# A four-layer trunk in which the retention's output product is computed head by head by Strassen's algorithm

## Chip, cores and metric

One core of a Trainium2 chip. The metric is the time of one execution of the program in microseconds on the device, the median of three runs; lower is better.

## The reference

Four residual layers; the token mixer of layer i is number i mod 3: retention (layers 0 and 3), a conformer convolution (1), a short gated convolution (2). Each mixer is followed by a squared-ReLU MLP, with a norm ahead of and behind every sublayer. All in float32, 512 tokens of width 1024. What the change touches is the last line of the retention mixer, `y @ w_out`:

```python
def retention_mixer(x, positions, w_in, gn_g, w_out):
    q, k, v, g = jnp.split(x @ w_in, [D_MODEL, 2 * D_MODEL, 2 * D_MODEL + RET_VDIM], axis=-1)
    ...                                   # 4 heads: q, k of 256, v, g of 512 columns each
    q = apply_rotary(q, cos, sin)
    k = apply_rotary(k, cos, sin) * (RET_DK ** -0.5)
    y = chunkwise_retention(q, k, v)      # 512 x 4 x 512
    mean = jnp.mean(y, axis=-1, keepdims=True)
    var = jnp.mean(jnp.square(y - mean), axis=-1, keepdims=True)
    y = ((y - mean) * lax.rsqrt(var + LN_EPS)).reshape(bsz, s, RET_VDIM) * gn_g.astype(F32)
    y = (jax.nn.silu(g.astype(F32)) * y).astype(x.dtype)
    return y @ w_out                      # 512 x 2048 times 2048 x 1024
```

## The kernel before

**Precision.** TensorE multiplies in a reduced float32 format, so every operand is held as a high part and a low part and every product is three matmuls (`mm3`: high by high, high by low, low by high). A high part is a ScalarE copy, the low part a VectorE subtraction of it from the value (`split`; `high` with `flush` is the same with the subtraction put off until the next copy).

**Weights.** `piece_list` writes out by hand the order in which weight pieces of 128 x 1024 are used. `fetch_hi` (ScalarE, line 289 or 284) and `fetch_lo` (VectorE, 302 or 298) split a piece; seven split pieces are held (`W_BUFS`), two raw ones. A piece that is used adds one to `owed`; `settle`, called just ahead of the next use, issues the owed fetches at that place of ScalarE's and VectorE's program. A raw tile is loaded by a DMA on SP's queue when the raw tile two before it has been split. A "fast" piece is no raw tile: it is one of the seven weight forms of a Strassen round and is made from four blocks (`blk`) that lie in SBUF, by VectorE subtractions in place (`combine`, line 329).

**Order.** All five engines run their instructions in the order in which the Python program issues them. PSUM has eight banks, taken in turn.

**Rounds.** `fast_round` multiplies one group by Strassen's algorithm in the Winograd form, with tokens, contraction and output columns each cut in two: seven forms, each of 2 banks x 2 contraction tiles x 3 matmuls = 12 matmuls of 512 columns for a group of four tiles (an ordinary product has 96 for the same, the round 84). Each form's two banks are added into `f` in SBUF at one or two places each (line 1385, or line 1383, a ScalarE copy, where the place is still empty). `halves_of` makes the left forms from a pair of tiles: splits and four sums of 256 columns. `fast_end` makes the last two sums. The MLPs use rounds of 16 and 8 tiles with the last four hidden tiles as a short last round, the short convolution one round of four tiles.

**Retention** goes head by head: query and key tiles of the next head (`do_qk`), scores (`do_s`), the retention product of this head (`do_o`), gate tiles (`gate` of `next(g)`), statistics (`stats`, `newton`, line 895 and 896), four output tiles (`do_y`, lines 829, 831, then the split), the value product of the next head (`do_v`: 96 matmuls, then the evacuations at lines 750, 754, 756). In head 0 the gate tiles were computed earlier, all but one of which stands between `do_o` and the statistics; in heads 1 and 2 one gate tile stands there and three behind the statistics; in head 3 two ahead of `do_o`, one ahead of the statistics and one behind. The output product before: at head 2, heads 0 and 1 together in `out_round` (8 pieces, into `f`); at the end heads 2 and 3 in `out_final`:

```python
        short = len(slots) == 1
        if not short:
            banks = [self.bank() for _ in range(4)]
            for kp in range(4):
                ...
                self.ts_part(banks, piece, slots, kp, mode == "bias")
```

That part takes the left 512 output columns, with head 2's contraction tiles first; after it `block(b)` computes the right 512 columns of each 128 tokens. With one slot (`short`) it falls away and `block(b)` computes both halves of the columns. The norms of the boundary are interleaved with the blocks.

## Time and profile before

| | |
|---|---|
| median of 3 runs | 2529.47 us (2528.72 to 2529.48) |
| the profiled execution, its own time | 2531.34 us |
| its span, first to last instruction | 2529.4 us |
| busy: TensorE, VectorE, ScalarE, GpSimd | 99%, 70%, 49%, 9% |
| mean granted TensorE clock | 0.996 of full |
| DMA moved | 290.97 MB, mean 115 GB/s |

The span is that of one execution with the hardware profiler on; the other 1.9 us of its time lie around it. Busy shares are means over stages that have different limits.

### The profile page before, as it was taken

How to read it: one execution, taken by the hardware profiler on the slowest of the kernel's cores; microseconds unless marked ns; L12 is line 12 of the kernel's file. 1: busy time of each engine (PE TensorE's matmuls, PEld its weight loads, DVE VectorE, ACT ScalarE, POOL GpSimd, SP SyncE). 2: the span in 40 equal slices, each digit the busy share in tenths (PEclk: the TensorE clock that was granted, in tenths of full speed). 3: DMA queues.
4: the chain of work that ended last, by engine and by line, in shares of the span. 5: the costliest groups of instructions: out<-in, count | busy, mean ns of one | idle time of the engine just before them, and what ended most of it. 6: DMA issues, size and time to landing. Idle time of an engine off the chain costs nothing.

```text
span 2529.4 us, 31444 instructions
## 1 busy us (share of the span) xinstructions
PE 2506.8 (99%) x12245; PEld 2121.1 (84%) x12245; DVE 1777.3 (70%) x2361; ACT 1232.6 (49%) x1874; POOL 218.4 (9%) x248
## 2 busy tenths in 40 slices
PE   9999999999999999999999999999999999999998
PEld 8888889888888788888898898888988888888887
DVE  7665346897978978678776577788756534687686
ACT  3553444555446656544443365445444334465543
POOL 0000002000026920000010100000200000200000
PEclk9999999999999999999999999999999999999999
DMA  4323234324243523331332233313332222331313
GB/s 154 111 88 104 84 117 138 138 104 171 90 146 101 192 98 142 133 134 67 141 109 88 87 142 133 133 67 123 124 104 82 95 88 102 136 135 73 133 67 125
DMA packets 85029, 290.97 MB, mean 115 GB/s; under 512 B 9488, under 2 KB 11280, under 8 KB 84880
## 3 DMA queue, kind: packets, MB, share of 16 engines
q1 hardware_dynamic: 84880, 288.96, 32.5%
q8 instruction: 96, 1.57, 0.3%
q14 instruction: 53, 0.43, 0.1%
HBM read 265.79 MB, written 21.50 MB: 114 GB/s over the span
## 4 chain that ended last, share of the span: by engine, by line
PE 64%; DVE 2%; POOL 2%; ACT 1%; issue 1%; DMA 0%; DVEq 0%; POOLq 0%; SPq 0%; ACTq 0%
PE bank L364 12%; PE bank L363 12%; PE bank L366 12%; PE bank L355 9%; PE bank L353 9%; PE bank L354 9%; POOL tiny L423 1%; DVE x L455 1%; POOL tiny L426 0%; PE bank L471 0%; POOL pbuf L1132 0%; DVE xin L404 0%; ACT bnd L442 0%; DMA whi<-phase 0%; PE bank L523 0%
## 5 line engine op out<-in xcount | busy, mean ns | idle before, releaser
L363 PE MATMUL bank<-xin,whi 128*128 128x512 f32 (+1 forms) x2160 | 759.9, 361 | 0.0
L364 PE MATMUL bank<-xin,wlo 128*128 128x512 f32 (+1 forms) x2160 | 757.2, 360 | 1.1 <-DVE wlo L302 1.1
L302 DVE TENSOR_TENSOR wlo<-raw,whi 128x1024 fp32r<-128x1024 f32 x320 | 392.0, 1233 | 377.8 <-ACT whi L289 373.0
L289 ACT ACTIVATE whi<-raw 128x1024 fp32r<-128x1024 f32 x320 | 333.4, 1054 | 432.5 <-DMA raw<-wall 296.3
L366 PE MATMUL bank<-xin,whi 128*128 128x512 f32 (+1 forms) x2160 | 475.2, 359 | 0.0
L364 PEld LDWEIGHTS bank<-xin,wlo 128*128 128x128 f32 x2160 | 409.5, 190 | 62.4 <-DVE wlo L302 1.9
L363 PEld LDWEIGHTS bank<-xin,whi 128*128 128x128 f32 x2160 | 409.6, 190 | 60.6 <-ACT xin L403 0.2
L366 PEld LDWEIGHTS bank<-xin,whi 128*128 128x128 f32 x2160 | 372.8, 189 | 60.5
L284 ACT ACTIVATE whi<-blk 128x1024 fp32r<-128x1024 f32 x203 | 210.8, 1053 | 153.9 <-DVE blk L329 144.3
L298 DVE TENSOR_TENSOR wlo<-blk,whi 128x1024 fp32r<-128x1024 f32 x203 | 247.0, 1220 | 30.1 <-ACT whi L284 27.2
L423 POOL TENSOR_SCALAR tiny<-tiny,tiny 128x1 f32<-128x1 f32 x32 | 50.0, 1564 | 1445.2 <-ACT tmp L442 1443.9
L1385 DVE TENSOR_TENSOR f<-f,bank 128x512 f32<-128x512 f32 x242 | 155.8, 679 | 0.0
L1285 ACT ACTIVATE tmp<-bank 128x512 f32<-128x512 f32 x128 | 74.6, 583 | 74.4 <-PE bank L366 74.4
L1132 POOL TENSOR_TENSOR pbuf<-pbuf 128x512 f32<-128x512 f32 x69 | 100.5, 1471 | 21.5 <-ACT pbuf L1129 18.3
L353 PE MATMUL bank<-whi,y 128*128 128x512 f32 x256 | 99.9, 390 | 0.0
L355 PE MATMUL bank<-whi,y 128*128 128x512 f32 x256 | 99.6, 389 | 0.0
L353 PE MATMUL bank<-whi,xin 128*128 128x512 f32 x256 | 99.6, 389 | 0.0
L354 PE MATMUL bank<-wlo,xin 128*128 128x512 f32 x256 | 99.6, 389 | 0.0
L354 PE MATMUL bank<-wlo,y 128*128 128x512 f32 x256 | 99.6, 389 | 0.0
L355 PE MATMUL bank<-whi,xin 128*128 128x512 f32 x256 | 99.6, 389 | 0.0
L353 PE MATMUL bank<-whi,far 128*128 128x512 f32 x256 | 99.6, 389 | 0.0
L354 PE MATMUL bank<-wlo,far 128*128 128x512 f32 x256 | 99.6, 389 | 0.0
(233 smaller groups left out, 4190.9 us busy)
## 6 DMA issues: line engine op xcount, KB each, us to landing
raw<-wall SPq DMA_DIRECT2D x320, 512.0 KB, 3.5
blk<-wall SPq DMA_DIRECT2D x116, 512.0 KB, 5.5
park<-x SPq DMA_DIRECT2D x20, 512.0 KB, 6.4
x<-park SPq DMA_DIRECT2D x20, 512.0 KB, 4.6
bnd<-norm_g SPq DMA_DIRECT2D x16, 512.0 KB, 8.2
phase<-tmp SPq DMA_DIRECT2D x32, 256.0 KB, 2.0
x<-x_in SPq DMA_DIRECT2D x8, 512.0 KB, 7.0
whi<-phase SPq DMA_DIRECT2D x8, 512.0 KB, 7.2
```

The source lines that it names most:

```text
L284: nc.scalar.activation(hi, self.form_of(c, n), AF.Copy)
L289: nc.scalar.activation(hi, self.raws[i], AF.Copy)
L298: lambda: nc.vector.tensor_sub(lo, self.form_of(c, n), hi.bitcast(F32))]
L302: nc.vector.tensor_sub(lo, self.raws.pop(i), hi.bitcast(F32))
L353: nc.tensor.matmul(out, ah, bh, start=start, stop=False)
L354: nc.tensor.matmul(out, ah, bl, start=False, stop=False)
L355: nc.tensor.matmul(out, al, bh, start=False, stop=stop)
L363: self.nc.tensor.matmul(out, wh[:, c], x, start=kt == 0, stop=False)
L364: self.nc.tensor.matmul(out, wl[:, c], x, start=False, stop=False)
L366: self.nc.tensor.matmul(out, wh[:, kt * P:(kt + 1) * P], self.xin[:, 1, kt, t0:t1], start=False, stop=kt == 7)
L1132: nc.gpsimd.tensor_tensor(accs[c], accs[c], pbuf[:, slot, :], op=ALU.add)
L1385: nc.vector.tensor_add(f, f, bank)
```

## The change

Heads 0, 1 and 2 are each multiplied as a Strassen round of four tiles, issued directly behind the value product of the next head. For that, each head loads the first four blocks of its output weights (`load_four`) at its start, its output tiles come in the order 0, 2, 1, 3, so that pairs are complete early, and `halves_of` makes the forms; the middle forms lie in the buffer that the scores had (`st`). The seven "fast" pieces of a head follow its successor's value pieces in the list. Head 3 is left as one slot for `out_final`, with four ordinary pieces. `halves_of` forms its sums in the two tiles themselves where it took two temporary tiles before, in the MLPs and the short convolution too. The two 16 KB buffers `h` become one of 16 KB (`h`) and two of 8 KB (`h2`); the other users (MLPs, both convolutions, the first weight tiles) are renamed accordingly (those parts of the diff are left out here).

```diff
 FAST = len(GROUPS)
 FORMS = (1, 2, 5, 6, 3, 7, 4)
 SC_ORDER = (0, 2, 1, 3, 4, 5, 6, 7)
+Y_ORDER = ((0, 2, 1, 3),) * (NH - 1) + ((0, 1, 2, 3),)
 
 
 O_GN = 0
...
 
             def g(h, fts=range(4)):
                 for ft in fts:
-                    ws(w, j, 32 + 4 * h + ft)
+                    ws(w, j, 32 + 4 * h + Y_ORDER[h][ft])
 
             qk(0)
             g(0, range(G_EARLY[layer]))
...
             for h in range(NH):
                 if h + 1 < NH:
                     qk(h + 1)
-                if h == 2:
-                    ts("ret_w_out", j, range(4))
                 g(h, range(0 if h else G0, 4))
                 if h + 1 < NH:
                     v(h + 1)
-            ts("ret_w_out", j, range(4, 8))
+                    out.extend(("fast", layer, "ret_w_out", form, 0) for form in FORMS)
+            ts("ret_w_out", j, range(6, 8))
         elif kind == 1:
             nth = {}
             for step in ORDER.split():
...
         for q in range(FAST):
             out += [("ts", "mlp_w2", layer, *where) for _, where in blocks(q)]
     out += [("ts", "sc_w_out", 0, kp, c) for kp in range(2) for c in range(2)]
+    out += [("ts", "ret_w_out", j, kp, c) for j in range(2) for kp in range(6) for c in range(2)]
     return out
+
+
+class Parts:
+
+
+    def __init__(self, tiles):
+        self.tiles = tiles
+
+    def __getitem__(self, key):
+        return self.tiles[key[1]][(key[0], *key[2:])]
 
 
 class Plan:
...
 
     def bank(self):
         return self.psum.tile([P, 512], F32, tag="bank", name=self.nm("bank"))
+
+    def four(self, name, second=0):
+
+        if not second:
+            return self.big.tile([P, 2, 4, S], F32R, tag="h", name=self.nm(name))
+        return Parts([self.big.tile([P, 4, S], F32R, tag="h2", bufs=2, name=self.nm(name)) for _ in range(2)])
 
     def tmp(self, n=512, dt=F32):
         return self.tp.tile([P, n], dt, tag="tmp", name=self.nm("tmp"))
...
             nc.vector.scalar_tensor_tensor(t, bank, -0.5, r, op0=ALU.mult, op1=ALU.mult)
             col = O_GN + 16 * j + 4 * h + dv
             nc.vector.scalar_tensor_tensor(t, t, small[:, col:col + 1], gate, op0=ALU.mult, op1=ALU.mult)
-            self.high(hs[h][:, 0, dv, :], hs[h][:, 1, dv, :], t)
+            if h + 1 == NH:
+                self.high(hs[h][:, 0, dv, :], hs[h][:, 1, dv, :], t)
+            elif dv < 2:
+                hs["upper"] = t
+                self.halves_of(t, None, dv, *hs[h])
+            else:
+                self.halves_of(hs["upper"], t, dv - 2, *hs[h])
 
         def gate(bank):
             t = self.tmp()
...
             gs.append(gate(next(g)))
         st = do_s(0)
         for h in range(NH):
+            y = self.four("y")
+            if h + 1 == NH:
+                hs[h] = y
+                for n in range(2):
+                    self.fast_end(n)
+            else:
+                side = self.big.tile([P, 2, D], F32, tag="h2", bufs=2, name=self.nm("side"))
+                end = self.big.tile([P, 2, 2, 256], F32R, tag="h2", bufs=2, name=self.nm("end"))
+                blk = [side[:, n, :] for n in range(2)]
+                blk += [self.wp.tile([P, D], F32, tag="blk", bufs=2, name=self.nm("blk")) for _ in range(2)]
+                for k in range(4):
+                    self.blk[0, k // 2, k % 2] = blk[k]
+                self.load_four("ret_w_out", j, 2 * h)
+                hs[h] = [y[:, :, :2, :], y[:, :, 2:, :], None, end]
             if h + 1 < NH:
                 do_qk(tiles(4))
-            if h == 2:
-                self.out_round([hs[0], hs[1]], True)
-            hs[h] = self.big.tile([P, 2, 4, S], F32R, tag="h", bufs=2, name=self.nm("y"))
             if h:
                 g, gs = tiles(4), []
             if h + 1 < NH:
...
                 r = self.newton(*parts, LN_EPS)
                 if bank is not None:
                     gs.append(gate(bank))
-                for dv in range(4):
-                    if len(gs) <= dv:
+                mid = rp.tile([P, 2, 1152], F32R, tag="st", bufs=1, name=self.nm("mid"))
+                hs[h][2] = mid.rearrange("p l t -> p (l t)")[:, :2 * D].rearrange("p (l k t) -> p l k t", l=2, k=2)
+                for n, dv in enumerate(Y_ORDER[h]):
+                    if len(gs) <= n:
                         gs.append(gate(next(g)))
-                    do_y(h, dv, banks[dv], r, gs[dv])
-                self.flush()
+                    do_y(h, dv, banks[dv], r, gs[n])
                 v = do_v()
+                self.fast_round(hs[h], h == 0, 1)
                 st = do_s(h + 1)
             else:
                 gs = [gate(next(g)), gate(next(g))]
...
         src = self.x_in if layer == 0 else self.x_park
         for b in range(4):
             nc.sync.dma_start(self.x[:, b, :], src[b])
-        return [hs[2], hs[3]], "add"
+        return [hs[3]], "add"
 
     def newton(self, v, r0, t, eps):
 
...
             self.split(own[:, 0, i, near[0]], own[:, 1, i, near[0]], a[:, near[0]])
             return
         self.split(far[:, 0, i, :], far[:, 1, i, :], b)
-        s14, s23 = self.tmp(), self.tmp()
-        nc.vector.tensor_add(s14[:, near[0]], a[:, near[1]], b[:, near[1]])
-        nc.vector.tensor_sub(s23[:, near[0]], s14[:, near[0]], a[:, near[0]])
-        nc.vector.tensor_sub(s23[:, near[1]], a[:, near[0]], a[:, near[1]])
-        nc.vector.tensor_sub(s14[:, near[1]], b[:, near[0]], s23[:, near[0]])
-        self.split(own[:, 0, i, near[1]], own[:, 1, i, near[1]], s14[:, near[0]])
-        self.split(mid[:, 0, i, :], mid[:, 1, i, :], s23)
-        self.split(end[:, 0, i, :], end[:, 1, i, :], s14[:, near[1]])
+        a0, a1, b0, b1 = (v[:, c] for v in (a, b) for c in near)
+        nc.vector.tensor_add(b1, a1, b1)
+        nc.vector.tensor_sub(a1, a0, a1)
+        nc.vector.tensor_sub(a0, b1, a0)
+        nc.vector.tensor_sub(b0, b0, a0)
+        self.split(own[:, 0, i, near[1]], own[:, 1, i, near[1]], b1)
+        self.split(mid[:, 0, i, :], mid[:, 1, i, :], a)
+        self.split(end[:, 0, i, :], end[:, 1, i, :], b0)
 
     def fast_round(self, forms, first, groups):
 
```

## Rows read from the trace of the kernel before

**Rows 1.** Page, busy time of each engine, share of the span, instructions.

```profile
PE 2506.8 (99%) x12245; PEld 2121.1 (84%) x12245; DVE 1777.3 (70%) x2361; ACT 1232.6 (49%) x1874; POOL 218.4 (9%) x248
```

**Rows 2.** Waits of PE: line, releaser, us in total, times, longest us.

```profile
PE bank L1036 <- DVE conv L1112: 5.3, 1, 5.3
...
PE bank L364 <- DVE wlo L302: 1.1, 4, 0.5
```

**Rows 3.** Page, costliest groups: count, busy us, mean ns, idle before.

```profile
L353 PE MATMUL bank<-whi,y 128*128 128x512 f32 x256 | 99.9, 390 | 0.0
```

**Rows 4.** Timeline of PE, end of head 3, layer 0: start us, us.

```profile
365.13 1.98 PE L366 MATMUL bank<-xin,whi 128*128 128x512 f32 x8
366.94 0.39 PE L353 MATMUL bank<-whi,y 128*128 128x512 f32 x1
```

**Rows 5.** Timeline of DVE, same place.

```profile
365.89 1.23 DVE L302 TENSOR_TENSOR wlo<-raw,whi 128x1024 fp32r<-128x1024 f32 x1 [5.88 <-ACT whi L289]
367.04 0.69 DVE L895 SCALAR_TENSOR_TENSOR tmp<-tmp,tmp 128x512 f32<-128x512 f32 x1
...
375.31 1.48 DVE L416 TENSOR_TENSOR y<-tmp,y 128x512 fp32r<-128x512 f32 x2
```

**Rows 6.** Timeline of ACT, same place.

```profile
370.06 0.63 ACT L408 ACTIVATE y<-tmp 128x512 fp32r<-128x512 f32 x1 [2.29 <-DVE tmp L831]
```

**Rows 7.** Timeline of PE, end of head 3, layer 3.

```profile
2143.17 0.39 PE L353 MATMUL bank<-whi,y 128*128 128x512 f32 x1
```

**Rows 8.** Timeline of DVE, same place.

```profile
2151.54 1.47 DVE L416 TENSOR_TENSOR y<-tmp,y 128x512 fp32r<-128x512 f32 x2
```

**Rows 9.** Windows: us, busy (x) PE, PEld, DVE, ACT, POOL, PEclk, DMA, GB/s.

```profile
750.00:754.00 4.00, 2.39 (x22) 2.22 (x21) 2.42 (x3) 3.42 (x7) 2.96 (x3) 1.00 0.01 2
...
869.00:872.00 3.00, 0.00 (x0) 0.00 (x0) 3.00 (x3) 1.60 (x3) 2.92 (x3) 0.87 0.14 25
872.00:878.00 6.00, 5.63 (x14) 3.57 (x15) 6.00 (x9) 4.99 (x7) 5.76 (x4) 0.50 0.29 100
878.00:880.00 2.00, 2.00 (x17) 1.94 (x16) 1.93 (x3) 1.17 (x4) 1.84 (x3) 0.99 0.71 262
```

**Rows 10.** Timeline of DVE, head 0, layer 0: output tiles.

```profile
120.21 0.69 DVE L829 SCALAR_TENSOR_TENSOR tmp<-bank,tmp 128x512 f32<-128x512 f32 x1
...
126.97 1.48 DVE L416 TENSOR_TENSOR y<-tmp,y 128x512 fp32r<-128x512 f32 x2
```

**Rows 11.** Timeline of PE, first matmul behind head 1's value product.

```profile
137.06 0.39 PE L353 MATMUL bank<-qk 128*128 128x512 f32 x1
```

**Rows 12.** Timeline of ACT, evacuation of that value product.

```profile
136.70 0.58 ACT L750 ACTIVATE tmp<-bank 128x512 f32<-128x512 f32 x1
...
138.98 1.95 ACT L754 ACTIVATE v<-tmp,tiny 128x512 fp32r<-128x512 f32 x3
```

**Rows 13.** Timeline of ACT, short convolution, up to its round.

```profile
1310.00 1.06 ACT L289 ACTIVATE whi<-raw 128x1024 fp32r<-128x1024 f32 x1 [4.19 <-DMA raw<-wall]
...
1316.85 0.63 ACT L403 ACTIVATE z<-tmp 128x512 fp32r<-128x512 f32 x1 [3.15 <-DVE tmp L1261]
1318.58 0.42 ACT L403 ACTIVATE z<-tmp 128x256 fp32r<-128x256 f32 x1 [1.09 <-DVE tmp L1345]
...
1351.19 2.03 ACT L1383 ACTIVATE f<-bank 128x512 f32<-128x512 f32 x4
```

**Rows 14.** Timeline of DVE, same place.

```profile
1320.04 1.03 DVE L404 TENSOR_TENSOR side<-tmp,side 128x512 fp32r<-128x512 f32 x2
...
1343.88 1.22 DVE L298 TENSOR_TENSOR wlo<-blk,whi 128x1024 fp32r<-128x1024 f32 x1
1345.02 1.22 DVE L329 TENSOR_TENSOR blk<-blk,blk 128x1024 f32<-128x1024 f32 x1
...
1355.35 1.28 DVE L1385 TENSOR_TENSOR f<-f,bank 128x512 f32<-128x512 f32 x2
```

**Rows 15.** Timeline of DVE, value product behind head 1, layer 0.

```profile
209.54 1.23 DVE L302 TENSOR_TENSOR wlo<-raw,whi 128x1024 fp32r<-128x1024 f32 x1 [4.21 <-ACT whi L289]
```

More of the change, by code (lines that the diff above doesn't have):

```diff
@@ L948, in conformer @@
         c_all = self.big.tile([P, 8, S], F32, tag="f", name=self.nm("conv"))
-        ubuf = self.big.tile([P, 4 * D], F32, tag="h", bufs=2, name=self.nm("ubuf"))
-        pbuf = self.big.tile([P, 8, S], F32, tag="h", bufs=2, name=self.nm("pbuf"))
+        ubuf = self.big.tile([P, 4 * D], F32, tag="h", name=self.nm("ubuf"))
+        pbuf = [self.big.tile([P, 4, S], F32, tag="h2", bufs=2, name=self.nm("pbuf")) for _ in range(2)]
         nu = 7
@@ L1127, in prod @@
                     if t == 0:
-                        accs[c] = pbuf[:, slot, :]
-                    nc.scalar.activation(pbuf[:, slot, :], u_of(c)[:, t:t + S], AF.Copy, scale=weight(c, t))
+                        accs[c] = pbuf[slot // 4][:, slot % 4, :]
+                    nc.scalar.activation(pbuf[slot // 4][:, slot % 4, :], u_of(c)[:, t:t + S], AF.Copy, scale=weight(c, t))
                 def padd(c=c, slot=slot):
-                    nc.gpsimd.tensor_tensor(accs[c], accs[c], pbuf[:, slot, :], op=ALU.add)
+                    nc.gpsimd.tensor_tensor(accs[c], accs[c], pbuf[slot // 4][:, slot % 4, :], op=ALU.add)
                 plan.job(("prod", c, t), "ACT", 0.61, deps, prod, after=c)
@@ L1205, in silu @@
                 if c % 4 == 0:
-                    slots.append(self.big.tile([P, 2, 4, S], F32R, tag="h", bufs=2, name=self.nm("z")))
+                    slots.append(self.four("z", c // 4))
                 ln[c] = slots[c // 4][:, 0, c % 4, :], slots[c // 4][:, 1, c % 4, :], self.tmp()
@@ L1234, in short_conv @@
         src = self.tiles(first)
-        z = [self.big.tile([P, 2, 4, S], F32R, tag="h", bufs=2, name=self.nm("z")) for _ in range(2)]
+        z = [self.four("z", n) for n in range(2)]
         own, far = z[0][:, :, :2, :], z[0][:, :, 2:, :]
@@ L1295, in mlp @@
             n = 2 * GROUPS[q]
-            far = self.big.tile([P, 2, 4, S], F32R, tag="h", bufs=2, name=self.nm("far"))
+            far = self.four("far")
             if n < 4:
@@ L1299, in mlp @@
             else:
-                own = self.big.tile([P, 2, 4, S], F32R, tag="h", bufs=2, name=self.nm("own"))
+                own = self.four("own", 1)
             mid = end = None
@@ L1324, in mlp @@
             self.fast_round((own, far, mid, end), q == 0, GROUPS[q])
-        hid = self.big.tile([P, 2, 4, S], F32R, tag="h", bufs=2, name=self.nm("hid"))
+        hid = self.four("hid", 1)
         self.x = self.big.tile([P, 4, D], F32, tag="x", name=self.nm("x"))
@@ L1482, in build @@
             self.r1, self.r2, self.turned = {}, {}, {}
-            self.early = big.tile([P, 4, D], F32, tag="h", bufs=2, name="early")
+            self.early = big.tile([P, 4, D], F32, tag="h", name="early")
             for b in range(2):
```

## Prediction

> **What bounds the kernel now.** I read the busy times first: TensorE is busy in 99% of the span, VectorE in 70%, ScalarE in 49% [rows 1]. A busy TensorE need not be a TensorE that never waits, so the waits of TensorE come next: the longest single one is 5.3 us in the conformer, and the waits for split weights come to 1.1 us in four places [rows 2]; none lies in a retention layer. Matmuls of 512 columns follow each other there every 0.227 us (eight of them from 365.13 to 366.94) [rows 4]. So in retention the time is the number of matmuls, as long as nobody makes TensorE wait. The change takes matmuls away and adds work and hurry on VectorE and ScalarE; the question is which TensorE waits it makes.
>
> **What it removes.** The output product has 768 matmuls of 512 columns in both layers: three groups of 256 [rows 3], 384 a layer, 96 for each head. A Strassen round of one head has 7 forms of 12, so 84. Three heads in two layers save 6 x 12 = 72 matmuls, at 0.227 us 16.3 us (8.2 a layer). That is the most the change can give.
>
> **What it adds off TensorE, per layer.** Weight tiles to split: before 16, after 21 form pieces and 4 plain ones, so 9 more pairs of a ScalarE copy and a VectorE subtraction; in the short convolution's round, which has the same shape, the next operation follows such a subtraction 1.14 us later [rows 14]. Twelve weight sums (4 a round, the same 1.14 us). Evacuations: 20 per round at 0.6 to 0.7 us (two took 1.28 [rows 14]), in head 0's round 8 of them on ScalarE, whose four came to 2.03 us [rows 13]. Together some 65 us more for VectorE in a layer of about 390 us. On the average there is room: at head 1 it idles 4.21 us before a subtraction that recurs with each 5.4 us weight tile [rows 15]. The tile sums in place are the same four operations on the same operands, each behind a subtraction that already waits for ScalarE's copy; I cost them at nothing, in the MLPs and the short convolution too, with fewer temporary tiles as the only possible gain. The transfers are as many as before: 4 tiles and 12 blocks for 16 tiles a layer. The 12 blocks go ahead of raw tiles on SP's queue, four at a time; a late raw tile made ScalarE wait 4.19 us in the short convolution, which loads four blocks the same way, and no TensorE wait follows [rows 2, 13]. Seven prepared pieces hide it: nothing, bounds 0 and 2 us a round (inside the bounds of the rounds below).
>
> **The tail of head 3: 7.4 us a layer.** Today, when the last gate tile is through, TensorE goes on at 366.94 with head 2's output tiles [rows 4], which have long been there. Behind this cover VectorE and ScalarE finish head 3: its Newton steps start at 367.04, the first high half is copied at 370.06, the last low half is done at 375.31 + 1.48 = 376.79 [rows 5, 6]. The cover is two weight pieces of 24 matmuls, 10.9 us to 377.8: it fits by one microsecond. After the change head 2 is already finished, and the next instruction on TensorE is head 3's own block 0, which needs the first tile's halves at once and the fourth tile's low half in its 12th matmul. That matmul would run at 366.94 + 11 x 0.227 = 369.43 and can run at about 376.85: 7.4 us late. In layer 3 TensorE goes on at 2143.17 and the low half comes at 2151.54 + 1.47 = 2153.01 [rows 7, 8]: 7.4 us again. Nothing in the change makes the chain shorter. Two layers: 14.8 us, bounds 12 (if the weight split of 1.23 us ahead of the Newton steps goes elsewhere [rows 5]) and 18.
>
> **The clock behind it.** TensorE would stand still for nearly 4 us (366.94 to 370.7) and then run 12 matmuls in 6 us. The nearest row is the conformer's wait of 5.3 us: the granted clock falls inside it (0.87 of full in 869 to 872), stays at 0.50, the 1.2 GHz level, to 878 and is 0.99 in the next 2 us; with TensorE busy 5.63 of these 6 us about 2.8 us of work are lost [rows 9]. A wait of 1.8 us inside 750 to 754 left the clock at 1.00 [rows 9]. I take 2 us a layer, bounds 0 and 2.8: 4.0 us. The Trainium skill (TensorE: Matmul & The Clock Gate, section "HAM oscillation — how this bites in real kernels") says that a kernel whose matmul bursts are parted by waits pays a re-throttled start after each; by that rule head 0's round, whose waits I work out below, would pay as well, some 2 us more a layer, and the whole come out 4 us higher than by the row at 750 to 754. I keep the row.
>
> **Head 0's round: 7.5 us a layer.** Here no gate tile lies between the statistics and the value product, so the whole output chain and the preparation of the round's weights fall into the 21.8 us of the value product (96 matmuls), which ends at 137.06 [rows 11]. VectorE starts on the outputs at 120.21 [rows 10]. A pair of output tiles now costs: two operations 1.5 us, a half-width split (copy 0.42 [rows 13], then a subtraction, 0.8 together), two more operations 1.4, and the split with four sums that in the short convolution took from 1316.85 to about 1321.0 [rows 13, 14], 4.2 us. So 7.9 a pair, 15.9 for two: VectorE is through at 136.1 instead of 128.4 [rows 10]. Queued behind it on both engines, in the order of issue, are the value product's four weight fetches, now form pieces: four subtractions and three sums at 1.14 us, and 2.7 us in which VectorE waits for a copy that had to wait for a sum: until 146.8. The four evacuations of the value product are queued behind the last of these copies on ScalarE, at about 144.4 instead of 136.70 [rows 12]. TensorE has free banks for two forms (5.4 us, to 142.5) and then needs a bank of the value product: free at 145.0, so 2.5 us lost. From there VectorE and ScalarE stay behind: the first form's four copies come after the value's own copies, which took 138.98 to 141.5 [rows 12] and a weight copy (1.2 us lost), and each later form brings 1.14 us of weight split and two to four evacuations of 0.6 us against 2.72 us of matmuls, with raw tiles two deep: 0.9, 0.4 and, for the first query tile after the round, 2.9 us. Sum 7.9, taken as 7.5. Bounds: nothing (the short convolution's round ran with none [rows 2]) and 12. Two layers: 15 us.
>
> **Heads 1 and 2.** The same working with gate tiles between the output tiles puts the last split 9 us ahead of the round, and the value product's evacuations 0.5 us ahead of its end; VectorE falls some 5 us behind in the round, within what eight banks hold. Nothing, bounds 0 and 3 us each.
>
> **The boundary to the MLP** becomes the short form that the other boundaries have, with 1.1 us of waits for weights in four places [rows 2]: 0.3 a layer, 0.6, bounds 0 and 2.
>
> **Sum** against the profiled execution's own 2531.3 us: -16.3 + 14.8 + 4.0 + 15 + 0.6 = +18.1, so 2549.4. That execution lies 1.9 us above the median, 2529.5, so for the median 2547.6, said as 2548.
>
> **The rivals.**
> - *Only the tails cost.* For it: no round in this kernel makes TensorE wait [rows 2], and fetches or banks may run further ahead than I let them. Against: VectorE and ScalarE have no slack left at head 0. -16.3 + 14.8 + 4.0 + 0.6 = +3.1: 2533. Chance 0.19.
> - *Faster.* The tail's chain ends sooner or other matmuls lie behind it, so that waits and clock come to less than 8.2 us a layer, the point from which it decides. For it: a weight split of 1.23 us stands ahead of the Newton steps on VectorE [rows 5]. Against: the rows of both layers say 7.4 before any clock loss. With 0 to 3 us left a layer: 2513 to 2520. Chance 0.13.
> - *Every round lags.* Raw tiles arrive late behind the blocks and heads 1 and 2 take their 3 us each (12 in all), and the lower clock follows the waits of head 0 too (some 4): 2564, up to 2570. For it: two to four evacuations and a split per form are more than 2.72 us. Against: the banks' depth. Chance 0.18.
>
> My forecast has 0.50, by its own bounds 2538 to 2560. This kernel's measurement can't tell changes within 0.2%, 5 us, from none. Faster: 0.13, all from that rival. Same: 0.12, two thirds of the first rival. Slower: the rest, 0.75. The range leaves out the faster cases and the ends of the others: 2530 to 2568.
>
> **What would show it.** 768 - 72 = 696 matmuls in the output product. Tail: TensorE waits of about 7 us a layer for ScalarE's and VectorE's y, a granted clock of 0.50 for some us behind. Head 0: waits on ScalarE's evacuation of the value product, 2 to 3 us at the third form, and on the forms' evacuations later. Heads 1 and 2: none over 1 us. I am wrong if the tail shows less than 5 us, if head 0's round runs through, or if waits turn up in an MLP.

## The result: 1.0% slower, and the profile after

The changed kernel takes 2553.5 us (median of 4 runs, 2552.5 to 2555.0) against 2529.1 us: 1.0099 of the time before, 95% interval 1.0087 to 1.0111. The profiled execution took 2552.74 us, its span is 2551.0 us. Three views of it answer to what the prediction read. First the page's busy times, the answer to [rows 1]:

```profile
PE 2505.2 (98%) x12173; PEld 2111.4 (83%) x12173; DVE 1935.4 (76%) x2599; ACT 1259.2 (49%) x1928; POOL 224.8 (9%) x248
```

TensorE has 72 instructions fewer, as predicted, and is busy 1.6 us less where 16.3 us of work were taken away: a matmul at the lower clock lasts longer (0.63 us instead of 0.39 in the rows below) and counts as busy. VectorE is busy 158 us more. The groups of one of the three matmuls of a product (low by high, line, count, busy us, mean ns, idle before) show where the output product went, the answer to [rows 3]:

```profile
L372 PE MATMUL bank<-whi,mid 128*128 128x512 f32 x272 | 105.8, 389 | 0.0
L372 PE MATMUL bank<-whi,y 128*128 128x512 f32 x160 | 67.0, 419 | 2.0 <-DVE y L433 1.9
L372 PE MATMUL bank<-whi,end 128*128 128x512 f32 x136 | 52.9, 389 | 0.0
```

Of 256 on y there are 160 left; `mid` has 48 and `end` 24 more than before (224 and 112 there). 160 + 48 + 24 = 232, three times that 696. The mean of the group on y rose from 390 to 419 ns: these are the matmuls that run right behind waits. The waits of TensorE, against [rows 2]:

```profile
PE bank L370 <- ACT y L425: 7.3, 2, 3.6
PE bank L380 <- DVE f L1423: 6.8, 4, 2.4
PE bank L370 <- ACT tmp L767: 6.4, 2, 3.2
PE bank L1072 <- DVE conv L1148: 5.2, 1, 5.2
PE bank L488 <- DVE bnd L478: 5.0, 3, 2.0
PE bank L372 <- DVE y L433: 1.9, 5, 0.5
PE bank L381 <- DVE wlo L319: 1.4, 6, 0.5
```

Four of them are new, each in both retention layers: head 3's first block waits for ScalarE's copy of y (L425) and then for VectorE's low halves of it (L433), both in the tail; the third form of head 0's round waits for the evacuation of the value product (L767); a first query tile behind a round waits for the evacuation of a form (L1423). The waits in the conformer, for the norms (L478, 6.0 us before) and for the splits are much as before.

**Where the 21.6 us between the two spans lie** can be read from the starts of the first transposes of each boundary (us from the span's start; all are starts in the timeline of TensorE):

| stretch | before | after | longer by |
|---|---|---|---|
| up to the boundary behind layer 0's retention | 405.03 | 414.56 | 9.5 |
| that boundary and the MLP | 334.87 | 336.29 | 1.4 |
| boundary and conformer | 194.30 | 192.46 | -1.8 |
| from there to layer 3 | 847.70 | 847.69 | 0.0 |
| layer 3's retention | 399.35 | 411.46 | 12.1 |
| from there to the end | 348.2 | 348.5 | 0.3 |

The conformer's -1.8 is not the change's: two kernels below, which change nothing there (`before_rev`, `inplace`), take 192.8 and 192.5 us for it too; it is the profiled execution of before that lay 1.8 us longer there, and that execution is 2.2 us above its median. The profiled execution of `cover_g21_late`, 2.6 us above its median, takes 194.3 us for it as well.

**The tail**, layer 0 and layer 3, on TensorE, ScalarE and VectorE (start us, us, engine, line; against [rows 4 to 8]):

```profile
388.07 1.98 PE L383 MATMUL bank<-xin,whi 128*128 128x512 f32 x8
393.69 0.50 PE L370 MATMUL bank<-whi,y 128*128 128x512 f32 x1 [3.64 <-ACT y L425]
...
400.02 0.63 PE L371 MATMUL bank<-wlo,y 128*128 128x512 f32 x1
400.44 0.63 PE L372 MATMUL bank<-whi,y 128*128 128x512 f32 x1
...
393.00 0.63 ACT L425 ACTIVATE y<-tmp 128x512 fp32r<-128x512 f32 x1 [2.29 <-DVE tmp L848]
...
389.98 0.69 DVE L931 SCALAR_TENSOR_TENSOR tmp<-tmp,tmp 128x512 f32<-128x512 f32 x1
...
398.26 1.47 DVE L433 TENSOR_TENSOR y<-tmp,y 128x512 fp32r<-128x512 f32 x2
...
2175.34 1.98 PE L383 MATMUL bank<-xin,whi 128*128 128x512 f32 x8
2180.96 0.79 PE L370 MATMUL bank<-whi,y 128*128 128x512 f32 x1 [3.64 <-ACT y L425]
...
2187.72 0.63 PE L372 MATMUL bank<-whi,y 128*128 128x512 f32 x1
...
2185.53 1.47 DVE L433 TENSOR_TENSOR y<-tmp,y 128x512 fp32r<-128x512 f32 x2
```

The last gate tile is through at 388.07 + 8 x 0.227 = 389.88. Head 3's 12th matmul, the one at 400.44, could run at 389.88 + 11 x 0.227 = 392.38. The low half that it needs is done at 398.26 + 1.47 = 399.73, so the chain is 7.35 us late; the matmul starts another 0.7 later and the matmuls follow each other every 0.43 us, which is the lower clock. In layer 3 the same reckoning gives 2187.00 against 2179.66: 7.34 us, and the half speed goes on for some three matmuls more than in layer 0.

**Head 0's round**, layer 0 (and its query tile in both layers), against [rows 10 to 12]:

```profile
141.20 0.39 PE L372 MATMUL bank<-whi,y 128*128 128x512 f32 x1
144.78 0.63 PE L370 MATMUL bank<-whi,y 128*128 128x512 f32 x1 [3.19 <-ACT tmp L767]
...
143.10 1.06 ACT L301 ACTIVATE whi<-side 128x1024 fp32r<-128x1024 f32 x1 [2.67 <-DVE side L346]
144.06 0.58 ACT L767 ACTIVATE tmp<-bank 128x512 f32<-128x512 f32 x1
...
119.14 0.69 DVE L846 SCALAR_TENSOR_TENSOR tmp<-bank,tmp 128x512 f32<-128x512 f32 x1
...
135.19 0.42 DVE L421 TENSOR_TENSOR end<-tmp,end 128x256 fp32r<-128x256 f32 x1
...
141.78 1.22 DVE L346 TENSOR_TENSOR side<-blk,side 128x1024 f32<-128x1024 f32 x1
...
164.78 1.23 DVE L319 TENSOR_TENSOR wlo<-raw,whi 128x1024 fp32r<-128x1024 f32 x1 [2.08 <-ACT whi L306]
...
167.25 0.50 PE L380 MATMUL bank<-xin,whi 128*128 128x512 f32 x1 [2.36 <-DVE f L1423]
...
1953.74 0.54 PE L380 MATMUL bank<-xin,whi 128*128 128x512 f32 x1 [2.31 <-DVE f L1423]
```

Read it backwards: the third form's matmul at 144.78 waits for the evacuation that starts at 144.06, this one is queued behind the weight copy at 143.10, and that copy waited 2.67 us for the weight sum at 141.78 on VectorE. The prediction had put that evacuation at 144.4.

**The granted clock** behind these waits (windows: us, then busy us and count of TensorE, its loads, VectorE, ScalarE, GpSimd, then PEclk, DMA share, GB/s; against [rows 9]):

```profile
145.00:149.00 4.00, 4.00 (x12) 3.10 (x12) 3.44 (x5) 4.00 (x11) 1.95 (x4) 0.57 0.00 0
167.00:171.00 4.00, 3.75 (x16) 3.12 (x17) 4.00 (x7) 0.06 (x1) 0.00 (x0) 1.00 0.54 159
394.00:398.00 4.00, 3.17 (x7) 1.67 (x6) 3.93 (x7) 1.26 (x2) 0.00 (x0) 0.52 0.90 342
...
1931.00:1937.00 6.00, 5.75 (x14) 4.49 (x15) 4.74 (x6) 6.00 (x15) 2.13 (x4) 0.50 0.01 3
1954.00:1958.00 4.00, 4.00 (x12) 3.09 (x12) 4.00 (x7) 0.15 (x1) 0.00 (x0) 0.57 0.53 186
```

The tail's first block runs at the 1.2 GHz level, as predicted. So does the start of head 0's round in both layers, and the query tile behind it in layer 3: that was not in the sum.

### The profile page after: what moved, and what is told of

It is laid out like the page before. It is cut to its first block, busy times and chain, and to the rows that moved or that the text cites. A ratio compares the mean times of both kernels' runs of the same rounds, so it can differ in the third digit from the quotient of the medians.

```text
span 2551.0 us, 31616 instructions
## 1 busy us (share of the span) xinstructions
PE 2505.2 (98%) x12173; PEld 2111.4 (83%) x12173; DVE 1935.4 (76%) x2599; ACT 1259.2 (49%) x1928; POOL 224.8 (9%) x248
## 4 chain that ended last, share of the span: by engine, by line
PE 80%; DVE 7%; POOL 5%; ACT 4%; issue 2%; DMA 1%; SPq 0%; POOLq 0%; DVEq 0%; ACTq 0%
PE bank L381 15%; PE bank L380 15%; PE bank L383 15%; PE bank L372 11%; PE bank L370 11%; PE bank L371 11%; POOL pbuf L1168 3%; POOL tiny L440 1%; DVE wlo L319 1%; DVE x L472 1%; POOL tiny L443 1%; DVE xin L421 1%; DVE f L1421 1%; ACT bnd L459 1%; DMA raw<-wall 0%
## 5 line engine op out<-in xcount | busy, mean ns | idle before, releaser
L319 DVE TENSOR_TENSOR wlo<-raw,whi 128x1024 fp32r<-128x1024 f32 x296 | 363.0, 1235 | 262.0 <-ACT whi L306 261.5
L306 ACT ACTIVATE whi<-raw 128x1024 fp32r<-128x1024 f32 x296 | 308.3, 1055 | 372.1 <-DMA raw<-wall 338.2
L301 ACT ACTIVATE whi<-blk 128x1024 fp32r<-128x1024 f32 x221 | 229.7, 1053 | 153.6 <-DVE blk L346 124.3
L315 DVE TENSOR_TENSOR wlo<-blk,whi 128x1024 fp32r<-128x1024 f32 x221 | 269.5, 1223 | 36.4 <-ACT whi L301 35.1
L1421 DVE TENSOR_TENSOR f<-f,bank 128x512 f32<-128x512 f32 x326 | 210.9, 684 | 0.0
L370 PE MATMUL bank<-whi,mid 128*128 128x512 f32 x272 | 106.1, 390 | 0.0
L371 PE MATMUL bank<-wlo,mid 128*128 128x512 f32 x272 | 105.9, 389 | 0.0
L372 PE MATMUL bank<-whi,mid 128*128 128x512 f32 x272 | 105.8, 389 | 0.0
L1168 POOL TENSOR_TENSOR pbuf<-pbuf,pbuf 128x512 f32<-128x512 f32 x69 | 100.4, 1470 | 20.1 <-ACT pbuf L1165 16.9
L370 PE MATMUL bank<-whi,far 128*128 128x512 f32 x256 | 99.7, 389 | 0.1
L370 PE MATMUL bank<-whi,xin 128*128 128x512 f32 x256 | 99.6, 389 | 0.0
L372 PE MATMUL bank<-whi,far 128*128 128x512 f32 x256 | 99.6, 389 | 0.0
```

Of the source, the lines that this page charges most:

```text
L301: nc.scalar.activation(hi, self.form_of(c, n), AF.Copy)
L306: nc.scalar.activation(hi, self.raws[i], AF.Copy)
L315: lambda: nc.vector.tensor_sub(lo, self.form_of(c, n), hi.bitcast(F32))]
L319: nc.vector.tensor_sub(lo, self.raws.pop(i), hi.bitcast(F32))
L370: nc.tensor.matmul(out, ah, bh, start=start, stop=False)
L371: nc.tensor.matmul(out, ah, bl, start=False, stop=False)
```

## The experiments

All times are against the kernel before, run on the same chip. "Cover" means matmuls that TensorE can run while the other engines finish what it needs next.

| kernel | what | us | ratio, interval |
|---|---|---|---|
| `cover` | two heads as rounds, head 2 back as cover | 2539.3 | 1.0041 (1.0026 to 1.0056) |
| `before_rev` | no rounds in retention, cover taken away | 2544.8 | 1.0060 (1.0044 to 1.0077) |
| `gate1` | two gate tiles of head 0 moved | 2549.2 | 1.0077 (1.0062 to 1.0092) |
| `g21` | one moved in layer 0, two in layer 3 | 2546.9 | 1.0069 (1.0055 to 1.0083) |
| `evac` | two weight fetches behind the value's evacuations | 2582.4 | 1.0211 (1.0196 to 1.0227) |
| `late` | two weight fetches behind the round | 2551.3 | 1.0092 (1.0078 to 1.0105) |
| `move` | a gate tile of head 3 moved | 2547.8 | 1.0075 (1.0061 to 1.0088) |
| `warm` | filler matmuls in the tail | 2557.6 | 1.0113 (1.0099 to 1.0127) |
| `inplace` | only the sums in place | 2529.1 | 1.0001 (0.9992 to 1.0010) |
| `g21_hold4_move` | three remedies | 2544.9 | 1.0065 (1.0052 to 1.0077) |
| `all3` | five remedies | 2536.5 | 1.0037 (1.0023 to 1.0050) |
| `cover_g21_late` | `cover` with two remedies | 2530.1 | 1.0005 (0.9996 to 1.0013) |

### The tail: is it the missing cover?

`cover` gives head 2 back to the ordinary last product:

```diff
-Y_ORDER = ((0, 2, 1, 3),) * (NH - 1) + ((0, 1, 2, 3),)
+Y_ORDER = ((0, 2, 1, 3),) * 2 + ((0, 1, 2, 3),) * 2
...
-                self.fast_round(hs[h], h == 0, 1)
+                if h < 2:
+                    self.fast_round(hs[h], h == 0, 1)
...
-        return [hs[3]], "add"
+        return [hs[2], hs[3]], "add"
```

> Only heads 0 and 1 are Strassen rounds; heads 2 and 3 go together through the ordinary last product, so that two weight pieces of head 2 (24 matmuls, 10.9 us) lie between the last gate tile and head 3's first block, as before the change. My theory (the tail's loss is the missing cover): against the changed kernel it pays 24 more matmuls (+5.4 us in two layers) and gets back the tails of 8.3 and 8.9 us and the boundaries (0.6): about 2541 us, and no TensorE wait for y in the tail. The rival 'the cost is the work added to VectorE and the transfers in general, a third for each round': one round in three less gives a third of 24 + 16 = 40 us back, 13 us, minus 5.4: 2545, with the tail's wait still there. The rival 'the tail waits for something else than the cover': 2559, the tail's wait unchanged. Head 0's round keeps its wait of about 3.3 us at the third form in all cases.

Measured 2539.3 us. No wait for y is left; head 0's 3.2 us wait is as it was (rows of TensorE's waits):

```profile
PE bank L371 <- ACT tmp L768: 6.4, 2, 3.2
PE bank L381 <- DVE f L1427: 5.9, 4, 2.5
```

The rival that puts the cost on the added work in general had 2545 with the tail's wait still there; it falls. But `cover` also takes a round's work off VectorE and ScalarE. `before_rev` does the reverse: it takes the cover from the kernel before and adds no work.

```diff
-            ts("ret_w_out", j, range(4, 8))
+            ts("ret_w_out", j, (6, 7, 4, 5))
...
-        return [hs[2], hs[3]], "add"
+        return [hs[3], hs[2]], "add"
```

> The kernel before, without any of Strassen's rounds in retention, in which the last product takes head 3's contraction tiles first and head 2's behind them (the same matmuls, in another order): it removes the cover of head 3's chain and nothing else. My theory: the tail loses what it loses in the changed kernel, 7.4 to 9 us a layer, so 2529 + 16 = about 2545 us. If the changed kernel's tail is slow because of its own added work on VectorE and ScalarE, and not for want of cover, this kernel stays within 3 us of before.

Measured 2544.8 us, and the same wait on TensorE in a kernel without Strassen's rounds in retention:

```profile
PE bank L353 <- ACT y L408: 7.3, 2, 3.6
```

So the tail's some 16 us are the price of the order alone. The change did not lengthen head 3's chain on VectorE (9.75 us from its Newton steps at 389.98 to 399.73, as 367.04 to 376.79 in [rows 5]); it took away the cover in front of its consumer.

### Cover that is no cover

```diff
-                gs = [gate(next(g)), gate(next(g))]
+                gs = [gate(next(g))]
...
                 for dv in range(4):
+                    if len(gs) <= dv:
+                        gs.append(gate(next(g)))
                     do_y(h, dv, banks[dv], r, gs[dv])
```

> The changed kernel with one gate tile of head 3 moved from ahead of its retention product to behind its statistics, so that 5.4 us more of TensorE time lie between the statistics and head 3's first block. My theory (the tail's loss is what is missing of cover): of 8.3 and 8.9 us, 5.4 to 7 come back in each layer, the first wait for y (3.6 us) falls to nothing, and with no wait over 2 us the granted clock stays at full: 2538 to 2543 us. If the chain of head 3 only starts later by as much, because VectorE or ScalarE is behind at that place, the tail keeps its 8 us: 2553. If the retention product, which now starts 5.4 us sooner, waits for its scores, 3 us a layer are lost there: 2544 to 2548.

Measured 2547.8 us: 5.7 us back where 10 to 15 were expected. Timelines of TensorE, ScalarE and VectorE:

```profile
391.83 0.39 PE L370 MATMUL bank<-whi,y 128*128 128x512 f32 x1
...
397.86 0.80 PE L372 MATMUL bank<-whi,y 128*128 128x512 f32 x1 [3.38 <-DVE y L433]
...
394.38 0.58 ACT L859 ACTIVATE tmp<-bank 128x512 f32<-128x512 f32 x1
...
395.65 0.68 DVE L846 SCALAR_TENSOR_TENSOR tmp<-bank,tmp 128x512 f32<-128x512 f32 x1
...
397.12 1.47 DVE L433 TENSOR_TENSOR y<-tmp,y 128x512 fp32r<-128x512 f32 x2
```

The first block now starts at 391.83 without a wait, but 3.4 us are lost ahead of its ninth matmul, which needs the third tile's low half. The gate of the fourth output is the tile that was moved. That tile is through on TensorE at about 391.8, its SiLU is taken at 394.38 behind a weight copy, and the fourth output starts at 395.65. The third tile's low half is late with it, because `high` issues a low half only behind the copy of the next tile: the last two subtractions run together from 397.12. The cover had been an input of the chain it was to cover, which my expectation overlooked. The boundaries behind the tails, too, now wait for the norm (1.2 and 0.6 us in layer 0, 1.4 and 0.6 in layer 3; 0.1 in all at each in the changed kernel).

### The clock in the tail

```diff
+        if layer_end and short and self.ret_tail:
+            self.warm(48)
```

> The changed kernel with 48 small matmuls of the identity (128 columns each, results unused) on TensorE between the last gate tile and head 3's first block, where it waits 3.6 us: they fill most of the wait and keep TensorE's activity up, and leave the chain of head 3 as it is. My theory (2 us a layer of the tail were put down to the clock): the granted clock stays near full behind the wait and the 12th matmul comes at the end of the last low half, so 0.7 us come back in layer 0 and 1.5 to 2 in layer 3: 2550 to 2552 us. If the clock falls all the same, or if it cost nothing beside the waits for y, the time is the changed kernel's, 2553 to 2554; if the fillers delay the first block, it is longer.

Measured 2557.6 us. The 48 calls, which were to fill most of a wait of 3.6 us, ran as 96 matmuls of 0.11 us (TensorE's timeline):

```profile
390.34 10.88 PE L272 MATMUL bank<-ident 128*128 128x128 f32 x96
400.98 0.48 PE L370 MATMUL bank<-whi,y 128*128 128x512 f32 x1
```

Two windows of it, columns as above:

```profile
394.00:398.00 4.00, 4.00 (x38) 4.00 (x37) 3.93 (x7) 1.34 (x3) 0.00 (x0) 1.00 0.83 298
401.00:405.00 4.00, 4.00 (x20) 3.31 (x20) 1.34 (x2) 0.28 (x1) 0.00 (x0) 1.00 0.60 216
```

The fillers do hold the clock at 1.00, but the first block starts behind them only at 400.98, 7.3 us later than in the changed kernel, so the run says nothing of what a filler of the right length would give. The clock's share of the tail is therefore only read off the rows: about 1.0 us in layer 0 (0.7 from the last low half to the 12th matmul, and 0.3 in the slow ones behind it) and 1.6 in layer 3 (0.7 and 0.9). That is argued, not shown, and it differs between executions: in `g21` and `late`, whose tails are unchanged, the 24th matmul of the first block comes 9.4 to 9.6 us late in each layer, where the changed kernel's comes 8.3 and 9.0 us late. Behind the same 7.35 us of the chain that leaves 2.0 to 2.3 us.

### Head 0's round: cover, order, or amount?

```diff
-G0 = 3
+G0 = 1
```

> The changed kernel with two of head 0's gate tiles moved from ahead of its retention product to behind its statistics: the number of matmuls stays, but VectorE gets 10.9 us more of TensorE time between the statistics and the round. My theory (head 0's round waits because the chain from the statistics to the split of the forms has only the value product as cover): the waits of 3.35, 0.55 and 2.7 us and the low clock behind them go, some 8 to 11 us a layer: 2532 to 2538 us, with the wait at the third form under 1 us. If it is the number of evacuations and splits per form (the rival 'every round lags'), the waits in the round stay and the time with them: 2550 to 2554. If moving the gates only moves the wait ahead to the scores of head 0, the time stays too, with a new wait there of some 4 us.

Measured 2549.2 us: two of the three theories hold, in different layers. The third form waits in neither; the query tile's wait, which my theory had going too, stays in both (2.5 and 2.3 us). Between the first transposes behind layer 0 and those behind layer 3 the kernel takes 1781.5 us instead of 1787.9; 6.2 us of this gain are layer 3's retention (405.2 us against 411.5). Layer 0 lost them again ahead of its scores, which must now wait for ScalarE to evacuate head 0's own value product:

```profile
73.27 1.01 PE L793 MATMUL bank<-ends 128*128 128x128 f32 x3 [5.44 <-ACT tmp L767]
```

`g21` moves one tile in layer 0 (`G0 = {0: 2, 3: 1}`):

> The changed kernel with one gate tile of head 0 in layer 0 and two in layer 3 moved from ahead of its retention product to behind its statistics. Moving two in layer 0 had made a new wait of 5.4 us ahead of the scores, which is one gate tile's time; with one moved, that wait should be gone. My theory (head 0's round lacks cover between statistics and round, the amount decides): the wait at the third form goes in both layers, the later wait of the first query tile (2.7) stays in both as it did with two moved; layer 0 gains 3.4 and 1.7 of clock, layer 3 the 6.1 that it gained before: 2542 to 2544 us. If one tile's 5.4 us are not enough in layer 0, its third form still waits 1 to 3 us and the time is 2546 to 2548.

Measured 2546.9 us, the time of the second branch. Layer 0 has a bit of both waits (0.9 at the third form, 1.2 at the scores): 5.4 us more on one side are 5.4 us less on the other, and neither side has them to spare.

`evac` tests the order on ScalarE, where the evacuation stands behind weight copies:

```diff
             for kp in range(4):
-                self.settle()
+                if kp < 2:
+                    self.settle()
```

> The changed kernel in which the last two weight fetches of each value product are issued behind its evacuations instead of ahead of them, on ScalarE and VectorE, in all heads. My theory (the third form waits for a bank of the value product because ScalarE's evacuation is queued behind weight copies that wait for weight sums): the wait of 3.35 us at the third form goes to nearly nothing in both layers, and the clock stays up there; the later waits (0.55, 2.7) may grow, since the last forms are ready later: 2543 to 2551 us. If ScalarE would be late anyhow, because VectorE is through with the outputs only at 135.6, the wait stays above 2.5 us and the time at 2553.

Measured 2582.4 us, 29 us slower than the changed kernel. The wait that it was made for is gone; timelines of ScalarE and TensorE:

```profile
139.74 0.58 ACT L768 ACTIVATE tmp<-bank 128x512 f32<-128x512 f32 x1
...
151.45 1.06 ACT L301 ACTIVATE whi<-blk 128x1024 fp32r<-128x1024 f32 x1 [2.43 <-DVE blk L346]
152.41 2.04 ACT L1420 ACTIVATE f<-bank 128x512 f32<-128x512 f32 x4
...
153.53 0.80 PE L370 MATMUL bank<-whi,end 128*128 128x512 f32 x1 [6.14 <-ACT f L1420]
```

The evacuation starts at 139.74 instead of 144.06. But each form piece is a chain (copy, subtraction, sum, next copy) that takes 3.5 us from one copy to the next (147.97 to 151.45 here) while TensorE spends 2.7 us on a form. Two such pieces were pushed into the round, the first form's copies came 2.7 us later (152.41 instead of 149.74), and a bank was missing at the fifth form: 6.1 us. Heads 1 and 2, where the value product had had room for these pieces, paid 2.9 us each as well. So the order on ScalarE places the wait; it doesn't make it.

`late` puts off the two fetches ahead of the last two forms, with raw tiles that arrive late (VectorE's 2.08 us wait at 164.78); `late` names those two forms:

```diff
-                self.settle()
+                if form not in late:
+                    self.settle()
```

> The changed kernel in which the weight fetches that are due ahead of a round's last two forms are issued only behind the round, with the first query tile or the scores' successors. In the trace of the changed kernel the first query tile behind head 0's round waits 2.4 us for the evacuation of the sixth form, and VectorE does that evacuation 8 us after its matmuls, behind two weight splits of which one waits 2.1 us for ScalarE and that for a raw tile. My theory (evacuations are queued behind splits of raw tiles that arrive late): the wait of the query tile falls to under 0.5 us in heads 0 and 1, and with the clock behind it some 4 us a layer come back: 2544 to 2547 us. If VectorE is behind because of the amount of its work, the wait stays at 2 us or more and the time at 2551 to 2554; if the fetches that are put off are missed by the query tiles, waits for weights appear there and the time rises.

Measured 2551.3 us, no different from the changed kernel. The query tile's wait has gone, and waits of 1.6 to 1.7 us, with the lower clock behind, turn up 35 us later at head 1's statistics, which wait for ScalarE:

```profile
201.54 0.50 PE L837 MATMUL bank<-tmp,ones 128*128 128x512 f32 x1 [1.62 <-ACT tmp L420]
```

Three edits thus moved head 0's wait (ahead to the scores, on to a later form, on to the next statistics), and none in layer 0 made it go away. That what is behind by then is the sum of VectorE's and ScalarE's work from head 0's statistics on is argued from this, not shown: no run takes work away there and leaves the rest. Whether a third raw tile would relieve it wasn't tried.

### The sums in place

```diff
-        s14, s23 = self.tmp(), self.tmp()
-        nc.vector.tensor_add(s14[:, near[0]], a[:, near[1]], b[:, near[1]])
...
+        nc.vector.tensor_add(b1, a1, b1)
```

> The kernel before with nothing but the tile sums in the two tiles themselves, in the MLPs and the short convolution. I costed this edit at nothing: 2529, within 1.5 us of before. In the changed kernel's trace the sums are 0.46 us apart instead of 0.34, and the first MLP came out 0.7 us later; if that is theirs, four MLPs give up to 3 us: 2531 to 2532. If fewer temporary tiles help, 2526 to 2528.

Only the change's hunk of `halves_of` is put into the kernel before. Measured 2529.1 us, ratio 1.0001 (0.9992 to 1.0010): nothing, as costed.

### All remedies together

`g21_hold4_move` has three heads as rounds, the gate tiles of `g21` and `move`, and the last form of head 2 held back (left out here: that form's weight sum is now issued behind an ordinary piece, and head 3's tiles lie in the two small buffers):

```diff
-                self.fast_round(hs[h], h == 0, 1)
+                self.fast_round(hs[h], h == 0, 1, FORMS[:6] if h == 2 else FORMS)
...
+                self.fast_round(hs[2], False, 1, FORMS[6:])
+                for n in range(2):
+                    self.fast_end(n)
```

> Both remedies together: head 0's gate tiles moved by one (layer 0) and two (layer 3), one gate tile of head 3 moved behind its statistics, and the last form of head 2's round (12 matmuls, 2.7 us) held back until after head 3's last gate tile. The number of matmuls is that of the changed kernel. My theory: the tails lose 0 to 2 us each, head 0's round 2.7 and some clock in each layer, so 2553.5 - 10 - 15 = about 2528 us, from 2520 to 2531: between equal to the kernel before and 0.35% faster. If every round lags for the number of evacuations and splits, the waits turn up elsewhere and the time stays above 2540.

Measured 2544.9 us, not 2528. The tail's wait shrank to 1.3 us, but the boundary behind it got one of 4.6 to 4.9 us, because VectorE could not start the norm (its timeline):

```profile
405.25 1.23 DVE L467 TENSOR_TENSOR f<-f,bnd 128x1024 f32<-128x1024 f32 x1 [5.25 <-DMA bnd<-norm_g]
```

The norm's weights stand on SP's queue behind four loads of the residual, and these behind a raw tile whose turn now comes later: the residual's loads are issued from 394.48 instead of 390.47. `all3` issues the residual's loads ahead of head 3's gate tiles and adds `late`:

```diff
+                self.x = self.big.tile([P, 4, D], F32, tag="x", name=self.nm("x"))
+                for b in range(4):
+                    nc.sync.dma_start(self.x[:, b, :], xs[b])
                 gs = [gate(next(g))]
```

> Three heads as rounds, with gate tiles moved in heads 0 and 3, the last form of head 2 held back, the last two fetches of each round put off, and head 3's four loads of the residual issued ahead of its gate tiles. Without the last two edits this came to 2545, with a wait of some 4.8 us in each layer for the first transposes of the boundary, where VectorE waited 5.3 us for the norm's weights, a DMA that stands on SP's queue behind the residual's loads. My theory: that wait falls to 1 us or less, the query tile's wait of 2.7 goes: 2545 - 8 - 8 = 2529, from 2526 to 2534. If VectorE's own queue at the end (six adds, four weight splits and four output tiles) is what holds the boundary, the first transposes still wait 3 us or more: 2536 to 2540.

Measured 2536.5 us. That DMA wait is gone, and the first transposes wait 1.0 us; but the second and third still wait 1.4 and 0.6 in each layer, and head 1's statistics up to 2.9. The time is the rival's, 2536 to 2540, but its sign, 3 us or more at the first transposes, is not there: the DMA wait went as my theory had it, and the gain went into waits elsewhere.

`cover_g21_late` takes the diffs of `cover`, `g21` and `late` together, with two heads as rounds.

> Two heads as rounds, head 2 back as cover ahead of head 3 (2539 us measured), head 0's gate tiles moved by one in layer 0 and two in layer 3, and the last two fetches of each round put off: every TensorE wait that the change made and that the runs have named is answered. 48 matmuls fewer than the kernel before, 10.9 us. My theory: 2539 - 7 (gate tiles) - 8 (fetches) = 2524, from 2520 to 2530, so equal to the kernel before or up to 0.35% faster. If the put-off fetches do nothing: 2532. If rounds cost something that no wait shows, more than 2533.

Measured 2530.1 us, ratio 1.0005 (0.9996 to 1.0013): equal to the kernel before. Its tail is whole, and 48 matmuls (10.9 us) are saved, but the heads' waits take them back: the gaps on TensorE in layer 0 sum to some 6 us (1.1 at the scores, 1.1 at the third form, 1.6 at later forms and the scores of head 1, 2.4 at the statistics), in layer 3 to 3.5, all at statistics, and the rest is largely clock (0.72 of full in 1975 to 1981). No version beat the kernel before.

## Why the prediction was right, and where its terms were off

**Direction and places were right, the size by three quarters.** It said 2548, likeliest slower; the run gave 2553.5, 24.4 us above the kernel before. Against the profiled execution its sum was +18.1 us, and that execution of the changed kernel is 21.4 us longer, or 23 with before's long conformer set right. Part of the closeness is luck: head 0's round was put 2.4 us too high, and this hides as much of the 6 us of clock that the sum left out.

**Matmuls, -16.3.** 72 fewer, as costed. The work added on VectorE, some 65 us a layer, came to 79 (158 us in both).

**The tail's chain, 7.4 a layer.** 7.35 and 7.34. `before_rev` and `cover` show that it is the cover and nothing else. The rival "faster" needed this to come under 8.2 with the clock and fell.

**The clock in the tail, 2 a layer.** By the rows of this execution 1.0 and 1.6, within the bounds of 0 and 2.8; by those of `g21` and `late` 2.0 to 2.3. The size was about right, and no run isolates it.

**Head 0's round, 7.5 a layer.** The third form's wait was sized at 2.5 and came to 3.4. The evacuation seems to start where I had put it (144.06 against 144.4), but TensorE and VectorE both ran 1.1 us ahead of the kernel before at that place. Counted from VectorE's first output (119.14, and 120.21 in [rows 10]) it started 24.9 us later, not 24.2: the four output tiles with their forms took 16.5 us (to 135.61) instead of 15.9. Of the later ones, 1.2, 0.9 and 0.4 at the forms came to 0.6 in layer 0 and nothing in layer 3, and the query tile's 2.9 came to 2.7 in both. Waits together: 6.6 and 6.0.

**The clock behind head 0's waits, nothing.** This is the step that failed. I rested it on the wait of 1.8 us inside 750 to 754 that left the clock at 1.00 [rows 9], but TensorE stands longer here, 3.4 and 2.7 us, and the row did not reach that far. Nor was it the nearest row of the trace of before. Some ten microseconds behind it, at the same boundary, a wait of 1.95 us is followed by nearly 6 us at 0.50 (timeline of TensorE, then windows):

```profile
762.76 1.54 PE L471 MATMUL bank<-ident,bnd 128*128 128x128 f32 x6 [1.95 <-DVE bnd L461]
...
762.00:768.00 6.00, 5.24 (x25) 5.25 (x26) 4.49 (x6) 3.47 (x5) 0.00 (x0) 0.50 0.54 173
```

Ahead of the first of these waits TensorE had run without a gap (4.00 us busy in 746 to 750); ahead of the second it had stood for 0.54 us once before. So the trace that the prediction read already held a wait of under 2 us with the lower clock behind it, and nothing was the wrong price for head 0's longer ones.

Measured by the matmuls that followed each other in 0.43 us instead of 0.227: eight behind the third form in layer 0 (1.6 us), fourteen in layer 3 (2.9), and some nine behind layer 3's query tile (1.7): 6 us in all. The Trainium skill (TensorE: Matmul & The Clock Gate, section "HAM oscillation — how this bites in real kernels") had spoken for such starts, and the trace agrees at the third form, with 0.57 and 0.50 in the windows behind it, and at layer 3's query tile with 0.57, but not at layer 0's, with 1.00. The prediction had priced the rule at 4 us and set it aside.

**Heads 1 and 2, nothing.** Head 1's query tile waits 1.5 us in layer 0 and 0.6 in layer 3 (with the restart 1.8 and 1.0 us lost), head 2 not at all: inside the 0 to 3 that was left, but not nothing, and head 1's 1.5 breaks the sign "none over 1 us".

**Boundaries, 0.6.** With the stretches behind them 1.4 and 0.3 (0.7 to 1.0 for the first in `gate1`, `g21` and `late`); six waits for splits come to 1.4 us where four came to 1.1. One of these four does lie in a retention layer, at layer 3's first weights, which the prediction denied: 0.2 us at 1799.3, too little to matter.

**The sum by rows.** Layer 0: -8.2 + 8.2 (head 0 with clock) + 1.8 (head 1) + 8.3 (tail with clock) = +10.1; the trace shows +9.5, or +10.1 from the first transposes of the kernel on. Layer 3: -8.2 + 10.6 + 1.0 + 9.0 = +12.4 against +12.1. The rival "every round lags" was right in that the clock follows the waits of head 0 too, and wrong in its 12 us for heads 1 and 2.

## What to carry to other kernels

Before taking matmuls out of a stage, ask what each of them was hiding: here 48 matmuls of another head (10.9 us) stood in front of matmuls that wait for a chain of 9.8 us on two other engines [rows 5], and giving up that order cost about as much in a kernel without the change as with it. In layer 0, reordering a stage whose off-path engines seem to have no slack only moved the wait elsewhere; cover must be work that the chain itself doesn't need, and bring no queue of its own behind it. And a wait is to be priced with the lower clock behind it, as a range, and from all rows of waits near it in length, not from the one that cost nothing.

## What the runs showed of the hardware

The clock did not follow the length of a wait alone: the query tile's waits behind head 0's round are alike (2.36 us at 167.25, 2.31 at 1953.74), and the granted clock behind them is 1.00 in 167 to 171 and 0.57 in 1954 to 1958. It isn't the place either: `warm` and `move` issue the same instructions up to layer 0's query tile, wait there as long (2.27 and 2.44 us), and get the lower clock for part of the same window (0.71 and 0.73 of full on the mean; `warm`, then `move`):

```profile
167.00:171.00 4.00, 3.88 (x12) 3.12 (x13) 4.00 (x7) 0.03 (x1) 0.00 (x0) 0.71 0.48 162
167.00:171.00 4.00, 3.32 (x10) 2.65 (x11) 4.00 (x7) 0.40 (x1) 0.00 (x0) 0.73 0.42 134
```

So the same wait at the same place was followed by either level, and the 6 us of clock behind head 0's waits are those of one execution. What decides it was not isolated. And each small identity matmul of `warm` shows as two of 0.11 us: 48 calls took 10.9 us.
